# A diffusion-backbone layer on one Trainium2 core: the order of the loads in its first merge block, the place of a pool, and the queue of the result's loads and stores

## The chip, the core and the metric

The kernel runs on one core of a Trainium2 chip. Five engines run their own streams of instructions: PE (TensorE, the matmuls), DVE (VectorE), ACT (ScalarE), POOL (GpSimd) and SP (SyncE, which here only issues DMAs). An engine takes its instructions in the order in which they were built into its stream, so an instruction that waits holds everything behind it on that engine. A DMA is issued by an engine (here SP and POOL), its bytes move on 16 DMA engines that all issuers share, and the instruction that needs the data waits on a semaphore.

The metric is device time in microseconds (us). Before the change three runs gave 3526.43, 3517.88 and 3511.94 us; the median is 3517.88 us.

## What is computed

One layer on 2048 latent tokens and 256 context tokens of width 1024, float32 (cut from the reference):

```python
hx = modulate(rmsnorm(x, norm1_g), sh1, sc1)
px = hx @ w_in                                        # recurrent | Fourier | gate columns
qx = rwkv_inputs(centred_shift(px[..., :RWKV_COLS]), lp)
yx, _, _ = bidir_wkv(qx, Sf, Sb, True)                # RWKV-7 scan, both directions
fx = fourier_latent(px[..., FOURIER_START:GATE_START], rows)
r  = rwkv_output(yx, qx, lp)                          # group norm, bonus, gate, @ w_up_r
m  = sigmoid(gate_f) * (fx @ w_up_f) + sigmoid(gate_r) * r
x  = x + ga1 * (m @ w_out)
hx2 = modulate(rmsnorm(x, norm2_g), sh2, sc2)
x  = x + ga2 * ((silu(gate) * up) @ w_down)           # gate, up = split(hx2 @ w_gu)
return rmsnorm(x, final_norm_g)
```

## The kernel before

Products keep float32 accuracy by splitting each operand into a high part and a remainder and adding three matmuls (`mm3`, lines 269 to 271: high by high, high by low, low by high). A weight comes in as `wraw` (line 261, SP), ACT makes `whi` from it (line 262) and DVE `wlo` (line 263). One matmul is 128x128 by 128x512.

The part up to the end of the scan is the same in both kernels. The stages that the change touches come after it:

- **Merge.** The 2048 tokens are four blocks of 512, taken in the order 1, 2, 0, 3. For each block `normed(n, j)`, four times, loads 128 tokens of the two scan results and what goes with them (`gny`, `gnb`, `gnv`, `sg`), sums them (POOL), normalises them (DVE for even j, a long row of ACT instructions for odd j), transposes them on PE (`gnt`, line 1232), multiplies by the gate (`gng`, line 1239) and splits the result into `oh` and `ol`. For the first block this normalisation is done earlier; only `ready(i)` loads its results (`gnb`, line 1196). `c_merge(n, ct)`, eight times a block, loads a weight `wr` of 512 KB (two places) and three tiles of 256 KB, `gr`, `gf`, `fm` (eight places of the tag `t2` for all of them), does 12 matmuls into `pr`, and puts the merged value into `mh` and `ml`. `c_out(n, ct)`, eight times a block, multiplies that by `w_out` (24 matmuls into `po`) and adds the residual `x1` (the DMA `x`, 512 KB for two). The output product of one block is built beside the merge of the next.
- **Operands of the feed-forward product.** `Operands.build(k)` reads `x1` back, applies the second norm and makes seven sums and differences (`hB`/`lB`, `hT`/`lT`), in tiles of `t2`; POOL makes the last `lT` (line 1318). Six products of the first three up steps, `early`, need only the first two of the seven and are done at the end of this stage.
- **Up**, twice. For each of 22 steps four weights `wA` (line 1404, SP) are combined on DVE (line 1409) into seven, each split and multiplied; results go to DRAM from POOL (`u_dr`, line 1432).
- **Down**, four times, one for each block. 22 steps of `wraw<-w_down`, `u_`, 8 banks of PSUM (`pd`, line 1484). At its end the eight banks are read with `x1f` (loaded from DRAM, line 1508), the row sum gives `rsf`, and DVE multiplies (line 1524) into the result, which is stored (`out_T`, line 1525). The second and fourth down follow a first and a third at once. During the first, POOL loads and builds the operands of the second up.

Tiles live in pools that are laid out on a stack. The tag `t2` of the merge lives in the pool `eb`, beside the second set of `m` and `x1` tiles. The pool `ff`, which holds `wA`, `u_` and the like, is opened where `eb` was, so the first instruction that writes into `ff` waits for the last readers of what `eb` held there.

What sets the order: each engine's stream is laid out by a scheduler, which simulates a timeline and takes the instruction that it finds ready first; the source's order counts only for instructions that go through the `Pinned` engines of lines 50 to 59 (`PE`, `DV`, `AC`, `GP`, `SY`), which keep it among themselves. Pinned instructions carry line 59 in the profile, whoever calls them. Before the change the loads of the merge were laid out by the scheduler:

```python
for ct in range(8):
    c_merge(0, ct)
    if ct in (4, 6):
        normed(1, ct // 2 - 2)
normed(1, 2)
normed(1, 3)
```

Of the kernel before, what the change touches and what calls it, by code (L numbers as in the profile page):

```python
# [7 lines left out]
F32 = mybir.dt.float32  # L8
# [32 lines left out]
def layer_kernel(ctx: ExitStack, tc, I, out_T, dbg=None):  # L41
# [210 lines left out]
    nc.gpsimd.memset(emb, -math.log(2.0))  # L252
    wah = cst.tile([128, 16], F32, name="wah")
    nc.vector.tensor_scalar(out=wah, in0=vec[:, V_W0:V_W0 + 16], scalar1=0.5, scalar2=None, op0=ALU.mult)
    def load_w(src, K, other=None):
        hi = wp.tile([128, KT, 128], F32R, tag="whi", name="whi", bufs=2)
        lo = wp.tile([128, KT, 128], F32R, tag="wlo", name="wlo", bufs=2)
        for k0 in range(0, K, 4):
            k1 = min(K, k0 + 4)
            raw = other() if other and k0 else wp.tile([128, 4, 128], F32, tag="wraw", name="wraw", bufs=RW)[:, 0:k1 - k0, :]  # L260
            nc.sync.dma_start(raw, src[:, k0:k1, :])
            nc.scalar.activation(out=hi[:, k0:k1, :], in_=raw, func=AF.Copy)  # L262
            nc.vector.tensor_tensor(out=lo[:, k0:k1, :], in0=raw, in1=hi[:, k0:k1, :].bitcast(F32), op=ALU.subtract)  # L263
        return hi, lo
# [919 lines left out]
    def gt(tag, b, shape=(128, 512), dt=F32):  # L1184
        return GN[0].tile(list(shape), dt, tag=tag, name=tag, bufs=b)
# [7 lines left out]
    def ready(i):  # L1193

        yb = gt("gnb", 4)
        nc.sync.dma_start(yb, yb_dr[128 * i:128 * i + 128, :])
        oh_split(0, i, yb)

    def normed(n, j):

        i = 4 * TB[n] + j
        y, yb, v_, sg, s8 = gt("gny", 3), gt("gnb", 4), gt("gnv", 2), gt("sg", 3, (128, 128)), gt("s8", 4, (128, 4, 8))
        nc.sync.dma_start(y, y_dr[0][128 * i:128 * i + 128, :])
        nc.sync.dma_start(yb, y_dr[1][128 * i:128 * i + 128, :])
        nc.sync.dma_start(v_, bv_dr[i].rearrange("p t s -> p (t s)"))
        nc.sync.dma_start(sg, sg_dr[:, CTX + 128 * i:CTX + 128 * i + 128])
# [36 lines left out]
    def c_merge(n, ct):  # L1243
        tb = TB[n]
        if ct == 0:
            MHL[n] = [EP[n % 2].tile([128, KT, 512], F32R, tag=f"m{y}", name=f"m{y}{tb}") for y in "hl"]
        (mh, ml), (oh, ol) = MHL[n], OHL[n]
        w = gt("wr", 2, (128, KT, 128), F32R)
        nc.sync.dma_start(w.bitcast(F32), wr_dr[ct])
        gr, gf, fm = t2("gr"), t2("gf"), t2("fm")  # L1250
        nc.sync.dma_start(gr, g_dr[8 + ct][:, 512 * tb:512 * tb + 512])
        nc.sync.dma_start(gf, g_dr[ct][:, 512 * tb:512 * tb + 512])
        nc.sync.dma_start(fm, fm_dr[ct][:, 512 * tb:512 * tb + 512])
        nc.scalar.activation(out=gf, in_=gf, func=AF.Copy, bias=1.0)
        nc.gpsimd.tensor_tensor(out=gf, in0=gf, in1=fm, op=ALU.mult)
        pr = pcx.tile([128, 512], F32, tag="cx", name="pr")
        mm3(pr, (w[:, 0:4, :], w[:, 4:8, :]), lambda k: oh[:, k, :], lambda k: ol[:, k, :], 4, 512)
        nc.vector.scalar_tensor_tensor(out=gr, in0=gr, scalar=1.0, in1=pr, op0=ALU.add, op1=ALU.mult)
        nc.vector.tensor_tensor(out=gr, in0=gr, in1=gf, op=ALU.add)
        split(mh[:, ct, :], ml[:, ct, :], gr)  # L1260

    def c_out(n, ct, acc_):
        tb = TB[n]
        mh, ml = MHL[n]
        if ct == 0:
            X1T[n] = EP[n % 2].tile([128, KT, 512], F32, tag="x1", name=f"x1_{tb}")
            ACC[n] = acc_()
        x1, acc = X1T[n], ACC[n]
        if ct % 2 == 0:
            nc.sync.dma_start(x1[:, ct:ct + 2, :], XTv[:, ct:ct + 2, CTX + 512 * tb:CTX + 512 * tb + 512])  # L1270
        w = load_w(I["w_out"][ct], KT, (lambda: gt("wo", 3, (128, 4, 128))) if n < 3 else None)
        po = pcx.tile([128, 512], F32, tag="cx", name="po")
        mm3(po, w, lambda k: mh[:, k, :], lambda k: ml[:, k, :], KT, 512)
        nc.vector.scalar_tensor_tensor(out=x1[:, ct, :], in0=po, scalar=ga1h[:, ct:ct + 1], in1=x1[:, ct, :], op0=ALU.mult, op1=ALU.add)
        nc.gpsimd.dma_start(x1_dr[:, ct, 512 * tb:512 * tb + 512], x1[:, ct, :])
        q = t2("sqk") if ct else acc
        nc.scalar.activation(out=q, in_=x1[:, ct, :], func=AF.Square)
        if ct:
            nc.gpsimd.tensor_tensor(out=acc, in0=acc, in1=q, op=ALU.add)
# [56 lines left out]
            ready(ct)  # L1336
    for ct in range(8):
        c_merge(0, ct)
        if ct in (4, 6):
            normed(1, ct // 2 - 2)  # L1340
    normed(1, 2)
    normed(1, 3)
    acc_ = lambda: t2("acc")
    for ct in range(2):
        c_out(0, ct, acc_)
# [15 lines left out]
    for ct in range(8):  # L1361
        c_out(3, ct, lambda: fh.tile([128, 512], F32, tag="rs", name="acc3", bufs=3))
        if ct == 0:
            out_stats(2, t2("rs"))
        if ct % 2:
            ops0.build(ct // 2)
    early = {}
    for f in range(3):
        w = load_w(I["w_gu"][f], KT)
        early[f] = {}  # L1370
        for m, o in enumerate(OPS[:2]):
            ps = pcx.tile([128, 512], F32, tag="cx", name="e" + o) if f < 2 else pmm.tile([128, 512], F32, tag="mm", name="e" + o)
            mm3(ps, [x[:, 4 * m:4 * m + 4, :] for x in w], lambda k: ops0.X[o][0][:, k, :], lambda k: ops0.X[o][1][:, k, :], 4, 512)
            early[f][o] = ps
    eps.close()


    ff = fst.enter_context(tc.tile_pool(name="ff", bufs=1, side="right"))

    def tmp(name):  # L1380
        return ff.tile([128, 512], F32, tag="t2", name=name, bufs=8)

    def raw_(name):
        return ff.tile([128, 512], F32, tag="raw", name=name, bufs=6)
# [76 lines left out]
    def down(tb, between=None):  # L1461
# [41 lines left out]
        for ct in range(8):  # L1503
            for f in (FT - 2, FT - 1):
                mm(f, ct)
            x1 = tmp("x1f")
            X1.append(x1)
            nc.sync.dma_start(x1, x1_dr[:, ct, t0:t0 + 512])
            nc.vector.scalar_tensor_tensor(out=x1, in0=PD[ct], scalar=ga2h[:, ct:ct + 1], in1=x1, op0=ALU.mult, op1=ALU.add)
            q = ff.tile([128, 512], F32, tag="sq", name="sqf", bufs=2) if ct else acc  # L1510
            nc.scalar.activation(out=q, in_=x1, func=AF.Square)
            if ct:
                nc.vector.tensor_tensor(out=acc, in0=acc, in1=q, op=ALU.add)
# [6 lines left out]
        for k in range(KT):  # L1520
            if last:
                (nc.gpsimd if k in (1, 4, 6) else nc.vector).tensor_tensor(out=X1[k], in0=X1[k], in1=rs, op=ALU.mult)
            else:
                nc.vector.scalar_tensor_tensor(out=X1[k], in0=X1[k], scalar=vec[:, V_GF + k:V_GF + k + 1], in1=rs, op0=ALU.mult, op1=ALU.mult)
            nc.sync.dma_start(out_T[128 * k:128 * k + 128, t0:t0 + 512], X1[k])

    up(0, ops0.X, early, lambda: out_stats(3, fh.tile([128, 512], F32, tag="rs", name="rs3", bufs=3)))
    ops1 = Operands(1, raw_, nc.gpsimd)
# [112 lines left out]
```

## Time and profile before

| | |
|---|---|
| median of three runs | 3517.88 us (3511.94 to 3526.43) |
| the profiled execution's own time | 3525.59 us |
| its span, first to last instruction | 3523.8 us |
| mean granted clock of PE | 0.959 |
| busy in the span | PE 3259.1 us, PE's weight loads 2692.1, DVE 2359.7, ACT 1603.5, POOL 712.7 |
| first merge block | 1764.3 to 1837.1 us |
| other merge blocks, operands, early products | 1837.1 to 2141.8 us |
| first up, first down, second down | 2153.9 to 2571.4, from there to 2713.7, from 2721.3 on |

Busy times overlap, so they don't add up to the span. The granted clock is a share of full speed: 1.00 is 2.4 GHz and 0.50 is 1.2 GHz; a mean between them means that the stretch had some of both. A row of the table of stretches shows where PE stood still: the length of the stretch less PE's busy time.

### The profile page before, as it was taken

The page shows a single profiled execution, that of the slowest core. Times are in us where ns is not written, and L with a number is a line of the kernel's source. Part 1 is how long each engine was busy: PE and PEld are TensorE (multiplying, and loading weights), DVE is VectorE, ACT ScalarE, POOL GpSimd, SP SyncE. Part 2 cuts the span into 40 slices and gives each one's busy share as a digit, 9 for nine tenths or more (in the row PEclk, how much of TensorE's full clock was granted, in tenths as well). Part 3 has the DMA queues.
Part 4 walks back from the last instruction along what each step waited for, and adds up shares of the span by engine and source line. Part 5 has one row for each costly group of instructions (what it writes and reads, how often), then busy time and mean ns, then how long its engine had stood idle before and what let it go on. Part 6 is the DMA issues. An engine that isn't in the chain of part 4 may idle for free.

```text
span 3523.8 us, 56518 instructions
## 1 busy us (share of the span) xinstructions
PE 3259.1 (92%) x20598; PEld 2692.1 (76%) x20598; DVE 2359.7 (67%) x4404; ACT 1603.5 (46%) x3092; POOL 712.7 (20%) x1118
## 2 busy tenths in 40 slices
PE   7999899999988888999969998999998999999987
PEld 6787777877877777777747876888877888888865
DVE  7678578757657777666666568777774397776354
ACT  4768466557543444444555344333353343333332
POOL 2133232323222343222123342000120000000000
PEclk9999999999999888999979999999999999999998
DMA  6344655544444665777588864222264432223452
GB/s 230 107 158 157 209 196 168 186 127 157 156 167 134 169 186 167 209 237 208 163 303 299 243 197 130 90 84 84 84 207 161 137 117 81 84 86 105 148 171 89
DMA packets 309924, 563.37 MB, mean 160 GB/s; under 512 B 91632, under 2 KB 103152, under 8 KB 309648
## 3 DMA queue, kind: packets, MB, share of 16 engines
q1 hardware_dynamic: 265744, 420.66, 37.4%
q0 software_dynamic: 43904, 139.12, 12.2%
q8 instruction: 163, 2.67, 0.3%
q14 instruction: 113, 0.93, 0.1%
HBM read 406.93 MB, written 152.71 MB: 159 GB/s over the span
## 4 chain that ended last, share of the span: by engine, by line
PE 35%; issue 11%; DMA 7%; DVE 5%; ACT 1%; POOL 1%; SPq 0%; DVEq 0%; POOLq 0%; ACTq 0%
PE pd L1484 11%; PE pT L269 3%; PE pT L270 2%; PE pT L271 2%; PE pB L271 2%; PE pB L269 2%; PE pB L270 2%; PE pf L59 1%; PE po L269 1%; PE po L270 1%; PE po L271 1%; DMA wraw<-w_down 1%; PE xr L59 1%; DMA tb_dr<-Q 1%; PE qk L59 1%
## 5 line engine op out<-in xcount | busy, mean ns | idle before, releaser
L263 DVE TENSOR_TENSOR wlo<-wraw,whi 128x512 fp32r<-128x512 f32 x438 | 298.0, 705 | 366.0 <-ACT whi L262 357.3
L262 ACT ACTIVATE whi<-wraw 128x512 fp32r<-128x512 f32 x438 | 262.4, 626 | 446.9 <-PE pd L1484 192.3
L1484 PE MATMUL pd<-uh,whi 128*128 128x512 f32 x704 | 278.8, 396 | 23.8 <-ACT whi L262 22.1
L1484 PE MATMUL pd<-ul,whi 128*128 128x512 f32 x704 | 277.0, 393 | 0.0
L269 PE MATMUL pxps<-hh,whi 128*128 128x512 f32 (+2 forms) x720 | 249.7, 347 | 8.8 <-ACT whi L262 6.3
L1484 PE MATMUL pd<-uh,wlo 128*128 128x512 f32 x704 | 252.6, 391 | 1.4 <-DVE wlo L263 1.2
L270 PE MATMUL pxps<-hl,whi 128*128 128x512 f32 (+2 forms) x720 | 246.0, 343 | 5.3 <-DVE hl L59 4.1
L271 PE MATMUL pxps<-hh,wlo 128*128 128x512 f32 (+2 forms) x720 | 245.2, 346 | 4.8 <-DVE wlo L263 4.6
L269 PE MATMUL fps<-hh,whi 128*128 128x512 f32 (+1 forms) x688 | 248.9, 362 | 0.3
L271 PE MATMUL fps<-hh,wlo 128*128 128x512 f32 (+1 forms) x688 | 244.6, 356 | 0.8 <-DVE wlo L263 0.8
L270 PE MATMUL fps<-hl,whi 128*128 128x512 f32 (+1 forms) x688 | 243.2, 354 | 0.0
L1422 DVE TENSOR_TENSOR u<-u,pT 128x512 f32<-128x512 f32 x172 | 118.0, 686 | 127.4 <-PE pT L271 126.0
L1484 PEld LDWEIGHTS pd<-uh,whi 128*128 128x128 f32 x704 | 133.9, 190 | 58.7 <-ACT whi L262 27.7
L59 DVE TENSOR_TENSOR tm<-Q,AI 128x126 f32<-128x126 f32 (+22 forms) x558 | 150.2, 269 | 36.9 <-DMA AI<-ab_dr 20.4
L59 DVE TENSOR_TENSOR Q<-Q,tm 128x126 f32<-128x126 f32 (+22 forms) x558 | 154.0, 276 | 20.2
L269 PEld LDWEIGHTS pxps<-hh,whi 128*128 128x128 f32 x720 | 137.2, 191 | 29.1 <-ACT whi L262 8.6
L270 PEld LDWEIGHTS pxps<-hl,whi 128*128 128x128 f32 x720 | 137.0, 190 | 27.8 <-DVE hl L59 6.5
L1484 PEld LDWEIGHTS pd<-uh,wlo 128*128 128x128 f32 x704 | 132.7, 189 | 30.2 <-DVE wlo L263 2.6
L1484 PEld LDWEIGHTS pd<-ul,whi 128*128 128x128 f32 x704 | 133.9, 190 | 27.8
L271 PEld LDWEIGHTS pxps<-hh,wlo 128*128 128x128 f32 x720 | 136.8, 190 | 22.2 <-DVE wlo L263 6.3
L269 PEld LDWEIGHTS fps<-hh,whi 128*128 128x128 f32 x688 | 130.7, 190 | 22.6 <-issue 3.4
L271 PEld LDWEIGHTS fps<-hh,wlo 128*128 128x128 f32 x688 | 130.4, 190 | 22.7 <-issue 2.7
(760 smaller groups left out, 8673.6 us busy)
## 6 DMA issues: line engine op xcount, KB each, us to landing
wraw<-w_in SPq DMA_DIRECT2D x210, 256.0 KB, 3.2
wraw<-w_down SPq DMA_DIRECT2D x176, 256.0 KB, 2.9
wA<-w_gu SPq DMA_DIRECT2D x176, 256.0 KB, 2.7
BD<-bd_dr SPq DMA_DIRECT2D x36, 512.0 KB, 7.1
KR<-kr_dr SPq DMA_DIRECT2D x36, 512.0 KB, 7.8
wada<-w_ada SPq DMA_DIRECT2D x32, 512.0 KB, 4.0
wf<-wf_dr SPq DMA_DIRECT2D x32, 512.0 KB, 6.9
wr<-wr_dr SPq DMA_DIRECT2D x32, 512.0 KB, 6.2
```

The source lines that it names most:

```text
L59: return lambda *a, **k: tc.keep_in_program_order(f(*a, **k))
L262: nc.scalar.activation(out=hi[:, k0:k1, :], in_=raw, func=AF.Copy)
L263: nc.vector.tensor_tensor(out=lo[:, k0:k1, :], in0=raw, in1=hi[:, k0:k1, :].bitcast(F32), op=ALU.subtract)
L269: nc.tensor.matmul(ps, wh[:, k, :], xh(k), start=start and k == 0, stop=False)
L270: nc.tensor.matmul(ps, wh[:, k, :], xl(k), start=False, stop=False)
L271: nc.tensor.matmul(ps, wl[:, k, :], xh(k), start=False, stop=stop and k == K - 1)
L1422: nc.vector.tensor_tensor(out=o, in0=x, in1=y, op=ALU.add)
L1484: nc.tensor.matmul(PD[ct], x[:, ct, :], y, start=f == 0 and i == 0, stop=f == FT - 1 and i == 2)
```

## The change

Three things change. The first is the order of the loads in the first merge block: the loads of `c_merge(0, ct)`, of `ready`, of the next block's `normed` (now in `block_load`) and the weights and residual of the first two output steps go through `SY`, in the order in which the source calls them. The second is the place of `t2`: it gets a pool of its own, `et`, which stays open, so that `eb` holds only the `m` and `x1` tiles, and is closed ahead of the early products. The third is the queue of the result's loads and stores: `x1f` is loaded, and `out_T` of the first three downs stored, by POOL.

```diff
@@ load_w @@
-    def load_w(src, K, other=None):
+    def load_w(src, K, other=None, sy=nc.sync):
...
-            nc.sync.dma_start(raw, src[:, k0:k1, :])
+            sy.dma_start(raw, src[:, k0:k1, :])
@@ pools @@
+    et = fst.enter_context(tc.tile_pool(name="et", bufs=1, side="right"))
     eps = ctx.enter_context(ExitStack())
     eb = eps.enter_context(tc.tile_pool(name="eb", bufs=1, side="right"))
...
     def t2(name):
-        return eb.tile([128, 512], F32, tag="t2", name=name, bufs=8)
+        return et.tile([128, 512], F32, tag="t2", name=name, bufs=8)
@@ ready @@
-        nc.sync.dma_start(yb, yb_dr[128 * i:128 * i + 128, :])
+        SY.dma_start(yb, yb_dr[128 * i:128 * i + 128, :])
@@ normed @@
+    LD = {}
+
+    def block_load(n, j, sy=nc.sync):
+        i = 4 * TB[n] + j
+        y, yb, v_, sg = gt("gny", 3), gt("gnb", 4), gt("gnv", 2), gt("sg", 3, (128, 128))
+        sy.dma_start(y, y_dr[0][128 * i:128 * i + 128, :])
+        sy.dma_start(yb, y_dr[1][128 * i:128 * i + 128, :])
+        sy.dma_start(v_, bv_dr[i].rearrange("p t s -> p (t s)"))
+        sy.dma_start(sg, sg_dr[:, CTX + 128 * i:CTX + 128 * i + 128])
+        LD[n, j] = y, yb, v_, sg
...
+        if (n, j) not in LD:
+            block_load(n, j)
+        y, yb, v_, sg = LD[n, j]
@@ c_merge @@
+        sy = nc.sync if n else SY
         w = gt("wr", 2, (128, KT, 128), F32R)
-        nc.sync.dma_start(w.bitcast(F32), wr_dr[ct])
+        sy.dma_start(w.bitcast(F32), wr_dr[ct])
...
@@ c_out @@
+        sy = nc.sync if n or ct > 1 else SY
...
@@ the first block @@
         c_merge(0, ct)
-        if ct in (4, 6):
-            normed(1, ct // 2 - 2)
-    normed(1, 2)
-    normed(1, 3)
+        if ct in (1, 2, 4, 6):
+            block_load(1, {1: 0, 2: 1, 4: 2, 6: 3}[ct], SY)
+        if ct in (3, 4, 6, 7):
+            normed(1, {3: 0, 4: 1, 6: 2, 7: 3}[ct])
@@ before and after the early products @@
+    eps.close()
+    ff = fst.enter_context(tc.tile_pool(name="ff", bufs=1, side="right"))
     early = {}
...
-    eps.close()
-
-
-    ff = fst.enter_context(tc.tile_pool(name="ff", bufs=1, side="right"))
-
-    def tmp(name):
-        return ff.tile([128, 512], F32, tag="t2", name=name, bufs=8)
+
+
+
+    tmp = t2
@@ down @@
-            nc.sync.dma_start(x1, x1_dr[:, ct, t0:t0 + 512])
+            nc.gpsimd.dma_start(x1, x1_dr[:, ct, t0:t0 + 512])
...
-            nc.sync.dma_start(out_T[128 * k:128 * k + 128, t0:t0 + 512], X1[k])
+            (nc.sync if last else nc.gpsimd).dma_start(out_T[128 * k:128 * k + 128, t0:t0 + 512], X1[k])
```

In `c_merge` the three loads of `gr`, `gf` and `fm`, and in `c_out` the load of `x` and the call of `load_w`, use `sy` in the same way. Because lines were added, line numbers of the changed kernel are higher: the weights of up are line 1415 in place of 1404, `x1f` 1519 in place of 1508, `out_T` 1536 in place of 1525, the builds 1321 to 1333 in place of 1309 to 1321.

The first place is SP's stream at the start of the first merge block, just behind the load of `g` and the four loads of `gnb<-yb_dr`. Before:

```order
L1249 DMA wr<-wr_dr_122 128x1024
L1249 DMA wr<-wr_dr_123 128x1024
L1203 DMA gny<-y_dr_94 128x512
L1205 DMA gnv<-bv_dr 128x512
L1206 DMA sg<-sg_dr 128x128
L1203 DMA gny<-y_dr_94 128x512
L1205 DMA gnv<-bv_dr 128x512
L1251 DMA gr<-g_dr_81 128x512
L1252 DMA gf<-g_dr_73 128x512
L1253 DMA fm<-fm_dr_98 128x512
L1251 DMA gr<-g_dr_82 128x512
L1252 DMA gf<-g_dr_74 128x512
```

and with the change (loads through `SY` stand under line 59):

```order
L59 DMA wr<-wr_dr_122 128x1024
L59 DMA gr<-g_dr_81 128x512
L59 DMA gf<-g_dr_73 128x512
L59 DMA fm<-fm_dr_98 128x512
L59 DMA wr<-wr_dr_123 128x1024
L59 DMA gr<-g_dr_82 128x512
L59 DMA gf<-g_dr_74 128x512
L59 DMA fm<-fm_dr_99 128x512
L59 DMA gny<-y_dr_94 128x512
L59 DMA gnb<-y_dr_95 128x512
L59 DMA gnv<-bv_dr 128x512
L59 DMA sg<-sg_dr 128x128
```

A merge step's four operands now follow each other. In the rows behind these, the kernel before has `x`, `wo`, `wraw` of `w_out` between the operands of the eight steps; the changed one has seven loads of `x` (after the rows shown), one `block_load` after the operands of the third, fifth and seventh step, and the weights of `w_out` behind the eighth.

The second place is the end of the operands and the start of up. On SP, before:

```order
L261 DMA wraw<-w_gu 128x512
L1309 DMA x__22015<-x_dr 128x512
L261 DMA wraw<-w_gu 128x512
L261 DMA wraw<-w_down 128x512 x4
L1404 DMA wA<-w_gu 128x512 x4
L261 DMA wraw<-w_down 128x512 x2
L1404 DMA wA<-w_gu 128x512 x11
```

and with the change:

```order
L261 DMA wraw<-w_gu 128x512
L1321 DMA x__22018<-x_dr 128x512
L1415 DMA wA<-w_gu 128x512 x2
L261 DMA wraw<-w_gu 128x512
L1415 DMA wA<-w_gu 128x512 x3
L261 DMA wraw<-w_down 128x512 x2
L1415 DMA wA<-w_gu 128x512 x3
L261 DMA wraw<-w_down 128x512 x2
L1415 DMA wA<-w_gu 128x512
```

The loads of `wA` moved ahead of the last weight of the early products (`wraw<-w_gu`) and of the first weights of down (`wraw<-w_down`). On DVE, with the change (`lB` and `lT` belong to the last build, `wS`/`wA` of line 1420 are the combined weights):

```order
L1420 TENSOR_TENSOR wS<-wA 128x512
L1330 TENSOR_TENSOR lB_0_21562<-x__22018,hB_0_21561 128x512
L1433 TENSOR_TENSOR c_22167<-u_22153,eB_22068 128x512
L1420 TENSOR_TENSOR wA<-wA 128x512
L1333 TENSOR_TENSOR x__22010<-x__22010,x__22006 128x512
L263 TENSOR_TENSOR wlo<-wraw,whi 128x512 x2
L1330 TENSOR_TENSOR lT_0_21556<-t_22022,hT_0_21555 128x512
L1420 TENSOR_TENSOR wA<-wS,wA 128x512
L1438 SCALAR_TENSOR_TENSOR tg<-tg,c_22167 128x512
L1333 TENSOR_TENSOR x__22006<-x__22018,x__22010 128x512
L1330 TENSOR_TENSOR lT_0_21558<-x__22010,hT_0_21557 128x512
L1420 TENSOR_TENSOR wA<-wA 128x512
```

The four combinations of line 1409 (now 1420), which stood behind all rows of the last build and of the early products, now stand between them.

The third place is the end of the first down, where the second follows. On SP, before:

```order
L1475 DMA u__26939<-u_dr_19104 128x512
L1475 DMA u__26979<-u_dr_19105 128x512
L1525 DMA out_T<-x1f 128x512 x4
L1508 DMA x1f<-x_dr 128x512
L1525 DMA out_T<-x1f 128x512 x2
L1508 DMA x1f<-x_dr 128x512
L1525 DMA out_T<-x1f 128x512 x2
L261 DMA wraw<-w_down 128x512
L1508 DMA x1f<-x_dr 128x512
L261 DMA wraw<-w_down 128x512
```

and with the change:

```order
L1486 DMA u__26942<-u_dr_19104 128x512
L1486 DMA u__26982<-u_dr_19105 128x512
L261 DMA wraw<-w_down 128x512 x2
L1486 DMA u__27022<-u_dr_19106 128x512
L1486 DMA u__27062<-u_dr_19107 128x512
L261 DMA wraw<-w_down 128x512 x3
L1486 DMA u__27102<-u_dr_19108 128x512
```

The rows of `out_T` and `x1f` are gone from between the weights. They stand on POOL, with the change, at the same place (`lT` is the last row of the builds of the second up):

```order
L1330 TENSOR_TENSOR lT_1_25460<-x__26268,hT_1_25459 128x512
L1536 DMA out_T<-x1f 128x512 x4
L1519 DMA x1f<-x_dr 128x512
L1536 DMA out_T<-x1f 128x512 x2
L1519 DMA x1f<-x_dr 128x512
L1536 DMA out_T<-x1f 128x512
L1519 DMA x1f<-x_dr 128x512
L1536 DMA out_T<-x1f 128x512
L1519 DMA x1f<-x_dr 128x512 x5
```

and, where the first down begins and POOL builds those operands:

```order
L1443 DMA u_dr_19116<-u_25384 128x512
L1519 DMA x1f<-x_dr 128x512 x5
L1333 TENSOR_TENSOR t_25886<-x__25882,x__25874 128x512
L1321 DMA x__26065<-x_dr 128x512
L1519 DMA x1f<-x_dr 128x512
L1443 DMA u_dr_19116<-c_25404 128x512
L1519 DMA x1f<-x_dr 128x512
L1321 DMA x__26069<-x_dr 128x512
L1333 TENSOR_TENSOR x__25878<-x__25878,x__25870 128x512
L1321 DMA x__26073<-x_dr 128x512
L1321 DMA x__26077<-x_dr 128x512
```

In the kernel before the rows of `x1f` are not among these; the store of `u` is followed at once by `t`. Five loads of `x1f` now stand between them.

## Rows read from the trace of the kernel before

**Rows 1.** The page: its head, and busy time by engine.
```profile
span 3523.8 us, 56518 instructions
...
PE 3259.1 (92%) x20598; PEld 2692.1 (76%) x20598; DVE 2359.7 (67%) x4404; ACT 1603.5 (46%) x3092; POOL 712.7 (20%) x1118
```

**Rows 2.** Stretches: length; busy PE, PEld, DVE, ACT, POOL; clock, DMA share, GB/s.
```profile
1764.30:1837.10 72.80, 37.97 (x145) 30.00 (x146) 43.78 (x74) 38.67 (x122) 20.69 (x16) 0.72 0.92 334
1772.00:1824.00 52.00, 29.23 (x108) 22.42 (x108) 32.35 (x53) 26.16 (x79) 15.46 (x11) 0.72 1.04 382
1837.10:1908.00 70.90, 70.90 (x337) 59.09 (x335) 48.59 (x80) 36.64 (x89) 28.87 (x26) 1.00 0.78 257
1908.00:1917.00 9.00, 2.27 (x11) 2.21 (x11) 5.89 (x11) 6.30 (x25) 2.11 (x2) 0.65 1.04 397
2115.90:2141.80 25.90, 20.37 (x72) 13.86 (x72) 24.81 (x31) 17.16 (x29) 12.34 (x10) 0.93 0.38 122
2141.80:2153.90 12.10, 0.03 (x1) 0.06 (x1) 6.58 (x11) 4.75 (x8) 1.69 (x1) 0.69 0.63 196
2571.40:2575.00 3.60, 0.08 (x2) 0.08 (x1) 2.75 (x3) 1.91 (x4) 3.31 (x5) 1.00 1.01 342
2713.70:2721.30 7.60, 0.02 (x2) 0.01 (x1) 0.72 (x2) 1.26 (x2) 0.00 (x0) 0.67 0.92 270
2721.30:2728.00 6.70, 6.70 (x19) 5.32 (x20) 1.36 (x2) 0.63 (x1) 0.00 (x0) 0.61 0.99 364
3388.40:3395.70 7.30, 0.07 (x1) 0.07 (x1) 0.78 (x2) 1.26 (x2) 0.00 (x0) 0.76 0.96 315
```

**Rows 3.** What PE waited for in the first block: total, times, longest.
```profile
PE pr L269 <- DMA wr<-wr_dr: 12.1, 2, 9.8
PE gnt L1232 <- ACT gny L1221: 6.3, 1, 6.3
```

**Rows 4.** DMAs issued from 1764 to 1826 us: size, median time to landing.
```profile
x<-xT SPq DMA_DIRECT2D x8, 512.0 KB, 7.6
...
gnb<-y_dr SPq DMA_DIRECT2D x7, 256.0 KB, 5.4
gny<-y_dr SPq DMA_DIRECT2D x6, 256.0 KB, 5.9
...
wo<-w_out SPq DMA_DIRECT2D x5, 256.0 KB, 7.3
...
wraw<-w_out SPq DMA_DIRECT2D x2, 256.0 KB, 6.5
```

**Rows 5.** What SP's queue waited for from 1760 to 1837 us.
```profile
SPq L1206 <- PE gng L1239: 4.9, 1, 4.9
SPq L1249 <- PE gnt L1232: 3.6, 1, 3.6
SPq L626 <- DMA fm_dr<-ev: 3.5, 1, 3.5
```

**Rows 6.** Timeline ahead of up, SP's DMAs: start, duration.
```profile
2143.92 1.75 SPq L1404 DMA_DIRECT2D wA<-w_gu  x4
```

**Rows 7.** Timeline there, DVE; in brackets the idle time before, and its releaser.
```profile
2150.96 0.69 DVE L1409 TENSOR_TENSOR wS<-wA 128x512 f32<-128x512 f32 x1 [1.64 <-DMA wA<-w_gu]
```

**Rows 8.** Timeline at the end of the first down, DVE.
```profile
2710.87 1.28 DVE L263 TENSOR_TENSOR wlo<-wraw,whi 128x512 fp32r<-128x512 f32 x2
```

**Rows 9.** Timeline there, SP's DMAs.
```profile
2715.62 0.52 SPq L261 DMA_DIRECT2D wraw<-w_down  x1
```

**Rows 10.** The page's DMA issues over the whole program.
```profile
wraw<-w_down SPq DMA_DIRECT2D x176, 256.0 KB, 2.9
```

**Rows 11.** DMAs issued from 2563 to 2578 us.
```profile
u_dr<-u POOLq DMA_DIRECT2D x1, 256.0 KB, 5.2
```

**Rows 12.** Timeline at the start of the first down, POOL.
```profile
2564.25 0.56 POOL L1432 DMA_DIRECT2D u_dr<-u  x1 [2.66 <-DVE u L1431]
2566.73 3.25 POOL L1321 TENSOR_TENSOR t<-x__25879,x__25871 128x512 f32<-128x512 f32 x1 [1.92 <-ACT x__25879 L1311]
```

More of the change, by code (lines that the diff above doesn't have):

```diff
@@ L1195, in ready @@
         yb = gt("gnb", 4)
-        nc.sync.dma_start(yb, yb_dr[128 * i:128 * i + 128, :])
+        SY.dma_start(yb, yb_dr[128 * i:128 * i + 128, :])
         oh_split(0, i, yb)
-    def normed(n, j):
[L1201 to L1206, printed above, removed]
+    LD = {}
[7 more added lines that the diff above has]
+        LD[n, j] = y, yb, v_, sg
+    def normed(n, j):
+        if (n, j) not in LD:
+            block_load(n, j)
+        y, yb, v_, sg = LD[n, j]
+        s8 = gt("s8", 4, (128, 4, 8))
         nm, ss, nb = s8[:, 0, :], s8[:, 1, :], s8[:, 2, :]
@@ L1247, in c_merge @@
         (mh, ml), (oh, ol) = MHL[n], OHL[n]
+        sy = nc.sync if n else SY
         w = gt("wr", 2, (128, KT, 128), F32R)
-        nc.sync.dma_start(w.bitcast(F32), wr_dr[ct])
+        sy.dma_start(w.bitcast(F32), wr_dr[ct])
         gr, gf, fm = t2("gr"), t2("gf"), t2("fm")
-        nc.sync.dma_start(gr, g_dr[8 + ct][:, 512 * tb:512 * tb + 512])
-        nc.sync.dma_start(gf, g_dr[ct][:, 512 * tb:512 * tb + 512])
-        nc.sync.dma_start(fm, fm_dr[ct][:, 512 * tb:512 * tb + 512])
+        sy.dma_start(gr, g_dr[8 + ct][:, 512 * tb:512 * tb + 512])
+        sy.dma_start(gf, g_dr[ct][:, 512 * tb:512 * tb + 512])
+        sy.dma_start(fm, fm_dr[ct][:, 512 * tb:512 * tb + 512])
         nc.scalar.activation(out=gf, in_=gf, func=AF.Copy, bias=1.0)
@@ L1268, in c_out @@
         x1, acc = X1T[n], ACC[n]
+        sy = nc.sync if n or ct > 1 else SY
         if ct % 2 == 0:
-            nc.sync.dma_start(x1[:, ct:ct + 2, :], XTv[:, ct:ct + 2, CTX + 512 * tb:CTX + 512 * tb + 512])
-        w = load_w(I["w_out"][ct], KT, (lambda: gt("wo", 3, (128, 4, 128))) if n < 3 else None)
+            sy.dma_start(x1[:, ct:ct + 2, :], XTv[:, ct:ct + 2, CTX + 512 * tb:CTX + 512 * tb + 512])
+        w = load_w(I["w_out"][ct], KT, (lambda: gt("wo", 3, (128, 4, 128))) if n < 3 else None, sy)
         po = pcx.tile([128, 512], F32, tag="cx", name="po")
```

## The prediction

> **What bounds the kernel now.** I read the page's busy times first. PE is busy 3259.1 of 3523.8 us, 92% [rows 1], so PE sets the pace and an edit counts only where it shortens a time in which PE stands still. Everything up to 1764.3 us is the same in both kernels. Second I read the table of stretches for such times behind that point; the idle time is the length less PE's busy time [rows 2]. The first merge block has 72.80 - 37.97 = 34.8 us of it, the change to up 12.1, the start of the first down 3.6 at most, the two changes from one down to the next 7.6 and 7.2. These five places, 65 us together, are all that the change touches and that PE feels. The stretch behind the first block, for one, has no idle time in 70.9 us.
>
> Third I read what ended each of them. In the first block PE waits for `wr` and for `gny` [rows 3], links of chains that start with a load, and from 1772 to 1824 us the DMA engines are full (share 1.04 at 382 GB/s [rows 2]). So bytes are the limit there for 52 us, and in the last 13 us the chain through ACT. At the change to up, SP asks for `wA` only at 2143.92, 2.1 us after PE's last matmul [rows 6], and DVE starts on it at 2150.96 [rows 7]. At the change between downs DVE gives back the places of `wraw` at 2710.87 + 1.28 = 2712.15 at the latest [rows 8], but SP issues the load at 2715.62 [rows 9], behind `out_T` and `x1f`.
>
> **The change part by part.**
>
> *First block.* The loads through SY ask first for what the merge products need. Of the issues up to 1826 us these move behind the last merge operand: one `x` of 512 KB (eight before, seven now), five `wo` and two `wraw` of `w_out`, two `gny` and three `gnb` of the block after the next (the next one needs four of each) [rows 4]. That is 0.52 + 12 x 0.262 = 3.7 MB, at 382 GB/s 9.6 us. Besides, SP stood 3.5 us for the landing of a store of `fm_dr` [rows 5] that had two loads of `w_out` in front of it; these are gone, and I count 1.5 us of the 3.5. Sum -11. The bounds: -17, if in addition `gnt` no longer waits for `gny`, whose row of waits is 6.3 us [rows 3]; and 0, if the deferred bytes are paid for later. For that they need idle DMA time: from 1837.1 to 1908.0 the share is 0.78, so 15.6 us are idle, and 9.6 us fit [rows 2]. But the next 9 us are full (1.04) and PE is busy for 2.27 of them, so a part may come back there; -11 holds by the nearer row, and the rest of the merge I take as 0, from -4 to +7 (one more such hole of 9.00 - 2.27 = 6.7).
>
> *Place of `t2`.* `wA` waited for the last reader of a `t2` tile, POOL's last `lT`. Now it waits for the last reader of `x1` alone, the store and the square of the last output step, which come before the early products. Its loads move ahead of 2141.8, so the DMA leaves the path (its share there is 0.38 [rows 2]). What is late next is DVE: it is busy 24.81 of the 25.9 us of the early products [rows 2], and the combined weights, five operations of 0.69 us [rows 7] up to the first split weight, now stand between the rows of the last build and delay it by 3.4 us. So of the 12.1 us some 3.5 stay: -8.6, and with a shorter stop a little less time at the lower clock (0.69 in the stop): -9. Bounds: -14, the whole 12.1 and 2 us of clock; -3, if DVE's rows delay the early products by as much as they save behind them.
>
> *Queue of the result's loads and stores.* With `out_T` and `x1f` off SP's queue, `wraw` is issued at the release of its place, 2711.5 for the first (half of the 1.28 us of two operations [rows 8]), 4.1 us sooner than 2715.62 [rows 9]. The transfer itself stays slow, since the 4 MB of `out_T` and `x1f` still move. So 7.6 - 4.1 = 3.5 us stay and the gain is 4.1; behind the hole PE has 19 matmuls in 6.7 us at a clock of 0.61 [rows 2], where at full clock one takes 70.9 / 337 = 0.21 us on the mean of the stretch at 1837 us; (6.7 / 0.21 - 19) x 0.21 = 2.7 us are lost to the clock, and I count 1 of them back. That is -5, and the same at the second place (7.30 us, 0.07 busy [rows 2]): -10. Bounds: -17, both holes and clock wholly gone; 0, if the loads only share the same bytes per second sooner.
>
> Over the program `wraw<-w_down` lands 2.9 us after its issue [rows 10]; here PE goes on 5.7 us after it, at 2721.3 [rows 2, 9], one conversion by ACT included: the traffic costs some 2 us whoever issues it. The Trainium skill ("DMA: Bandwidth & Descriptors", section "Issuing engines are not separate DMA queues") says that transfers from all issuers run on the same 16 engines, and that spreading them only saves time on the sequencer. By that rule alone this part would be worth nothing; but the trace shows that it is SP's standing in line, 2711.5 to 2715.62, that counts here, which is the part that the rule leaves.
>
> *Start of the first down.* SP is rid of `x1f`, but POOL now issues five of them between the store of `u` and `t`, and the fifth waits for that store's landing, 5.2 us [rows 11]. So `t`, which started at 2566.73, starts behind 2564.25 + 5.2 = 2569.45 at the earliest [rows 12]: 2.7 us late, and ACT's `hT<-t` with it, on whose stream the `whi` stands that PE waits for. Against that the weights come sooner, and ACT does them ahead of the last `hT`. From -3.5 (the hole of 3.6 [rows 2] gone) to +4; I take -1.
>
> The stores from POOL behind up's `u_dr`, and the 32 loads, need about 0.56 us of POOL each [rows 12]; POOL is busy 20% of the span [rows 1], which hides them.
>
> Sum: -11 + 0 - 9 - 10 - 1 = -31 us. The profiled execution took 3525.59 us, 1.8 more than its span [rows 1]; it would take 3494.6. It is 7.7 us above the median of 3517.88, and the median goes to 3487.
>
> **The rivals.**
>
> *The bytes come back.* The deferred bytes have to land before the second block is through; if the hole at 1908 us grows by what the first block gains, 11 us are gone: 3517.88 - 20 = 3498. For: share 1.04 there. Against: 15.6 idle us before it, and PE busy without a gap until then [rows 2].
>
> *The change between downs gains nothing.* POOL issues `out_T` and `x1f` at the same time as SP issues `wraw`, and all land in 7 us as before: 3517.88 - 21 = 3497. For: shares of 0.92 and 0.96 in the holes [rows 2]. Against: `wraw` would stand first and not last.
>
> *The place of `t2` does not do what it says.* If DVE, not the load, ends the wait for up, the sum is -22, 3496. For: DVE's 24.81 of 25.9 us. Against: DVE idle for 1.64 us just before `wS` [rows 7].
>
> *SP stands in fixed order: slower.* In the pinned order a `block_load` whose place isn't free holds all operands behind it. SP's waits for PE were 4.9 and 3.6 us, for one `sg` and one `wr` [rows 5]; if each of the four block loads costs both, 34 us of standing are set against the gain of 11, +23, and the weights of `w_out`, later by that, open the hole of 6.7 us at each of the three blocks behind: +20. With the other terms, -20, that is +23: 3541. It decides once SP's lag exceeds the 15.6 idle us. For: seven loads of `x`, 3.7 MB, stand in front of the third step's weight. Against: those waits came when SP had run ahead and PE was busy with the steps before.
>
> **How the numbers follow.** The forecast has a chance of 0.55, the bytes that come back 0.15, no gain between downs 0.12, the place of `t2` 0.06, the fixed order 0.12 (in full strength or half). What a measurement tells from no change is 0.5%, 17.6 us, so faster means below 3500.3. The forecast's own range by its bounds is 3470 to 3502. Faster: nearly all of 0.55, two thirds of the next three cases (all stand 2 to 4 us from the bound), 0.73 together. Slower: half of the last, 0.06; the same: 0.21. The low end is 3466, where all four terms reach their lower bounds (-17 - 14 - 17 - 3.5 = -51.5); the high end is 3512, where the first two rivals come together and part of the term on up fails as well.
>
> **What would show it.** First block: `po` starts near 1826 in place of 1837, with `wr` and `gr` of each step in a row and the share still near 1; if the hole at 1908 is longer than 9 us, the bytes came back. Up: `wA` issued before PE's last early product, and the first `pT` some 3.5 us behind it, released by DVE. Downs: `wraw` issued at the release by `wlo`, holes of 3 to 4 us. First down: `t` late by some 3 us. I am wrong if the sum over those five holes doesn't fall by about 30 us, and by much if PE gets holes between 1837 and 2115 that weren't there, or if SP waits for PE in the first block for longer than 8.5 us in all.

## The result, and the profile after

The changed kernel takes 3505.65 us in the median of 20 runs (3490.08 to 3513.58), the kernel before 3525.28 us in the median of 20 (3511.68 to 3535.59). The ratio is 0.9944 with a 95% interval from 0.9931 to 0.9958: 0.56% or 20 us faster, where 31 us were forecast. The page of the changed kernel begins

```profile
span 3510.5 us, 56527 instructions
...
PE 3268.3 (93%) x20598; PEld 2697.7 (77%) x20598; DVE 2358.7 (67%) x4404; ACT 1606.1 (46%) x3092; POOL 744.9 (21%) x1174
```

The two profiled spans differ by 13.3 us, but that is not the effect. The scan's last matmul ended at 1764.3 us before and at 1772.8 us after, although both kernels have the same instructions up to there. So the stages are compared from the scan's end on. The table is read off PE's timeline (start of the first or end of the last matmul of a kind), so the first down begins here with its first `pd`, at 2560.4 us before, and not with PE's stop at 2571.4; the last three columns are experiments with one part each, told below.

| stage, us | before | changed | order of loads alone | place of t2 alone | queue alone |
|---|---|---|---|---|---|
| scan's end to first `po` | 72.8 | 63.7 | 65.3 | 73.6 | 73.2 |
| first to last `po` | 278.8 | 283.7 | 283.3 | 276.2 | 280.4 |
| last `po` to first `pT` of up | 38.0 | 30.9 | 38.4 | 29.7 | 38.8 |
| first up | 406.5 | 404.6 | 406.2 | 405.4 | 405.8 |
| first and second down | 262.0 | 258.4 | 260.7 | 262.5 | 256.0 |
| second up | 419.8 | 419.8 | 419.8 | 419.8 | 419.8 |
| third and fourth down | 254.8 | 252.6 | 253.9 | 255.8 | 250.5 |
| last `pd` to the end | 26.9 | 24.1 | 26.7 | 26.7 | 23.8 |
| all behind the scan | 1759.5 | 1737.8 | 1754.3 | 1749.7 | 1748.4 |

Behind the scan the changed kernel is 21.7 us shorter. The table of stretches of the changed kernel answers to [rows 2]; its columns are the length, the busy time of PE, PEld, DVE, ACT and POOL, PE's granted clock, the DMA share and GB/s:

```profile
1772.80:1836.40 63.60, 34.26 (x132) 25.90 (x132) 36.45 (x62) 29.74 (x87) 18.57 (x15) 0.83 1.00 360
1836.40:2120.10 283.70, 268.63 (x1189) 220.98 (x1189) 178.83 (x275) 141.01 (x331) 108.29 (x97) 0.95 0.76 241
2120.10:2151.00 30.90, 22.05 (x73) 14.75 (x73) 30.62 (x41) 21.66 (x36) 15.19 (x10) 0.89 0.49 159
...
2708.00:2710.60 2.60, 0.62 (x3) 0.19 (x1) 0.69 (x1) 1.26 (x2) 2.31 (x5) 1.00 0.94 230
2716.30:2720.00 3.70, 0.12 (x2) 0.07 (x1) 0.08 (x1) 0.74 (x2) 1.07 (x2) 0.95 1.04 397
...
3379.90:3383.50 3.60, 0.02 (x1) 0.00 (x0) 0.71 (x2) 1.26 (x2) 2.09 (x4) 1.00 0.91 300
3389.20:3392.20 3.00, 0.14 (x2) 0.07 (x1) 0.09 (x1) 0.75 (x2) 0.54 (x1) 0.98 1.01 363
```

The first block still runs its DMA engines full (share 1.00). The stop of 12.1 us ahead of up is gone, but the early products in front of it take 30.9 us, with DVE busy for 30.62 of them. Each change between downs has two stops of PE (stretches in which it does nothing), 2 to 3.6 us each, where one of over 7 stood; the clock stays near 1.00 in them, where it was 0.67 and 0.76.

What PE waited for in the changed kernel's first block, beside [rows 3]:

```profile
PE pr L269 <- DMA gr<-g_dr: 9.0, 1, 9.0
PE gnt L1242 <- DVE gny L1239: 9.0, 2, 7.1
PE po L269 <- ACT whi L262: 5.7, 1, 5.7
PE pr L269 <- DMA wr<-wr_dr: 4.4, 6, 1.5
PE gnt L1242 <- ACT gny L1231: 1.4, 2, 1.0
```

The waits for `wr` fell from 12.1 to 4.4 us and the one for ACT's `gny` from 6.3 to 1.4. A new one stands at the end: `po` waits 5.7 us for `whi`, the weights of `w_out`, which now come last. SP's waits there answer to [rows 5]; it waited for PE once, for 1.5 us:

```profile
SPq L626 <- DMA fm_dr<-ev: 1.8, 1, 1.8
...
SPq L59 <- PE pr L271: 1.5, 1, 1.5
```

### The profile page after: what moved, and what is told of

It reads as the page before. It is cut to its first block, busy times and chain, and to the rows that moved or that the text cites. A ratio compares the mean times of both kernels' runs of the same rounds, so it can differ in the third digit from the quotient of the medians.

```text
span 3510.5 us, 56527 instructions
## 1 busy us (share of the span) xinstructions
PE 3268.3 (93%) x20598; PEld 2697.7 (77%) x20598; DVE 2358.7 (67%) x4404; ACT 1606.1 (46%) x3092; POOL 744.9 (21%) x1174
## 4 chain that ended last, share of the span: by engine, by line
PE 45%; DMA 5%; DVE 4%; issue 3%; ACT 1%; POOL 0%; SPq 0%; DVEq 0%; POOLq 0%; ACTq 0%
PE pd L1495 11%; PE pT L269 5%; PE pT L270 5%; PE pT L271 5%; PE pB L269 3%; PE pB L270 3%; PE pB L271 3%; PE po L269 1%; DMA wraw<-w_down 1%; PE po L270 1%; PE po L271 1%; PE pf L59 1%; PE qk L59 1%; PE pr L269 1%; DVE wlo L263 1%
## 5 line engine op out<-in xcount | busy, mean ns | idle before, releaser
L269 PE MATMUL pxps<-hh,whi 128*128 128x512 f32 (+2 forms) x720 | 250.5, 348 | 8.9 <-ACT whi L262 6.6
L269 PEld LDWEIGHTS pxps<-hh,whi 128*128 128x128 f32 x720 | 137.4, 191 | 29.7 <-ACT whi L262 9.1
## 6 DMA issues: line engine op xcount, KB each, us to landing
wraw<-w_in SPq DMA_DIRECT2D x210, 256.0 KB, 3.2
wA<-w_gu SPq DMA_DIRECT2D x176, 256.0 KB, 2.7
wraw<-w_down SPq DMA_DIRECT2D x176, 256.0 KB, 2.9
```

What stands on the lines that cost most here:

```text
L269: nc.tensor.matmul(ps, wh[:, k, :], xh(k), start=start and k == 0, stop=False)
```

## The experiments

Eleven kernels ran. A ratio is against the kernel before on the same chip, with its 95% interval.

**Each part alone.** Three kernels have the kernel before and one part of the change.

> Kernel before, with the fixed order of the loads in the first merge block alone. Theory 1 (the three parts add up, each as the trace of the changed kernel shows it): from the scan's last matmul to the first po 64 us in place of 72.8, then from the first po to the last 284 us in place of 279, the change to up and the downs as before; in all about 4 us faster. Rival (the bytes put off come back whole): the same first stretch, but the second longer by all of the 9 us; 0.

> Kernel before, with the pool of t2 and the earlier place of ff alone. Theory 1 (DVE is what the change to up now waits for): PE's stop of 12.1 us ahead of up is gone, the early products take 31 us in place of 26, and from the last po to the first pT 31 us in place of 38: 7 us faster. Rival (the longer early products of the changed kernel come from its other parts): the stop gone, the early products 26 us, 12 us faster.

> Kernel before, with x1f and out_T on GpSimd's queue alone. Theory 1 (wraw no longer stands behind them, but all bytes still land in the same time): at each change between downs two stops of PE of 2 to 4 us each in place of one of 7.6 and smaller ones; 3 us each and 6 us in all faster. Rival (the loads of x1f hold POOL's t at the start of the first down): the stop of 3.5 us there grows to 6 or more, and 3 us at most are left.

Measured: 0.9977 (0.9961 to 0.9993) for the order of the loads, 0.9984 (0.9965 to 1.0002) for the place of `t2`, 0.9988 (0.9972 to 1.0004) for the queue. The product is 0.9949, beside 0.9944 for all three, so the parts add up; the last two intervals hold 1. The stages tell more: behind the scan the parts gain 5.2, 9.8 and 11.1 us in their traces, 26.1 together, somewhat more than the 21.7 of the whole. For the queue the trace says 11 us and the ratio 4 (up to 10 by its interval); a trace is one execution, and which of the two is nearer the ratios leave open.

The order of the loads does what theory 1 says: 7.5 us less to the first `po`, 4.5 more from there to the last. The place of `t2`: no stop, early products 29.8 us in place of 25.9, 8.3 us less in all (7 expected), and so the longer early products are its own price. The queue: 6.0 and 4.3 us less in the two pairs of downs (3 expected for each), and 3.1 at the end, which no theory had. Theory 1 had two stops at each change between downs; there is one, of 3.0 and 3.4 us, and behind it none longer than 1 us. The start of the first down did not get slower: PE's stop there is 2.7 us.

**Does DVE set the pace of the early products?** The edit on the changed kernel; `lo` is not made:

```diff
-        w = load_w(I["w_gu"][f], KT)
+        hi = wp.tile([128, KT, 128], F32R, tag="whi", name="whi", bufs=2)
+        for k0 in (0, 4):
+            raw = wp.tile([128, 4, 128], F32, tag="wraw", name="wraw", bufs=RW)
+            nc.sync.dma_start(raw, I["w_gu"][f][:, k0:k0 + 4, :])
+            nc.scalar.activation(out=hi[:, k0:k0 + 4, :], in_=raw, func=AF.Copy)
+        w = hi, hi
```

> Changed kernel; the low part of the weights of the six early products is left out (the high part is used in its place), so DVE has six operations less there. Theory 1 (DVE sets the pace of the early products): from the last po to the first pT 26 us in place of 31. Rival (loads or ACT set it): 30 to 31 us as before.

Measured: 26.9 us from the last `po` to the first `pT` (theory 1: 26), where the other kernels with this place of `t2` have 29.5 to 30.9 (28.5 in one). In the changed kernel PE's waits in that stretch were

```profile
PE eB L271 <- DVE wlo L263: 5.6, 4, 2.0
PE eB L270 <- DVE lB L1330: 1.8, 1, 1.8
PE eB L269 <- ACT whi L262: 1.4, 3, 0.6
```

and without the six operations on DVE

```profile
PE eB L270 <- DVE lB L1330: 3.2, 2, 3.1
PE eB L269 <- ACT hB L1329: 2.4, 2, 1.8
```

So DVE sets most of the pace, and the last build's own rows, on DVE and ACT, are next.

**Are bytes the limit of the first block?** The seven early loads of `x` go behind the merge operands:

```diff
         if ct % 2 == 0:
-            sy.dma_start(x1[:, ct:ct + 2, :], ...
+            (SY if n < 2 else nc.sync).dma_start(x1[:, ct:ct + 2, :], ...
```

> Changed kernel, with all loads of x for the first two blocks in the fixed order too, so that the seven early ones (3.7 MB) go behind the operands of the eight merge steps. Theory 1 (bytes limit the first block: 3.7 MB at 382 GB/s are 9.6 us): the last pr ends 8 to 10 us sooner after the scan than 58 us; po then waits for its weights and starts 6 to 9 us sooner than 63.7. Rival (the chain from gny to ol, or two places of wr, sets the pace): 0 to 3 us sooner.

and, in a second kernel, the first weights of `w_out` come earlier as well:

```diff
         c_merge(0, ct)
+        if ct == 5:
+            W0.append(load_w(I["w_out"][0], KT, lambda: gt("wo", 3, (128, 4, 128)), SY))
```

> As x_late, and the weights of the first output step are loaded ahead of the operands of the last two merge steps. Theory 1 (po waits 5.7 us only because its weights are last in line): PE's stop ahead of po falls below 2 us, the merge products end 1 to 2 us later, po starts 3 us sooner than in x_late. Rival (all is one queue of bytes, whatever their order): po starts within 1 us of x_late.

Measured: 0.9923 (0.9897 to 0.9949) and 0.9932 (0.9909 to 0.9956), not to be told from the changed kernel's 0.9944. In the trace of the first the last `pr` ends 54.9 us after the scan (58.0 in the changed kernel, 60.4 with the order of loads alone), and `po` starts after 58.3: 5.4 us sooner, less than the 6 to 9 of theory 1 and more than the 0 to 3 of the rival. The last `pr` ended 3.1 us sooner than in the changed kernel, where theory 1 had 8 to 10. Its first block and PE's waits in it:

```profile
1763.00:1821.20 58.20, 33.03 (x132) 25.21 (x132) 34.96 (x63) 29.62 (x86) 19.40 (x15) 0.85 0.90 308
```

```profile
PE pr L269 <- DMA wr<-wr_dr: 11.4, 5, 2.6
PE pr L269 <- DVE ol L275: 9.4, 1, 9.4
PE po L269 <- ACT whi L262: 3.3, 1, 3.3
```

The DMA share is 0.90, so bytes no longer fill the whole block; PE waits five times, up to 2.6 us, for `wr`, which has two places. Both theories hold a part. With the weights earlier the stop ahead of `po` is gone and `po` starts after 56.2 us, 2 us sooner; but from the first to the last `po` it takes 288.6 us, 5 more, with a new stop of 3.3 us ahead of a `pr` 17 us into it. In this trace, what is taken from the one stop comes back behind it.

**What makes the two stops between downs?** The first attempt fixed the order of all that a down loads on SP:

```diff
-            w = load_w(I["w_down"][f], KT)
+            w = load_w(I["w_down"][f], KT, None, SY)
...
-            nc.sync.dma_start(r, u_dr[f][:, t0:t0 + 512])
+            SY.dma_start(r, u_dr[f][:, t0:t0 + 512])
...
+            if f >= FT - 10:
+                x1 = tmp("x1f")
+                X1.append(x1)
+                SY.dma_start(x1, x1_dr[:, len(X1) - 1, t0:t0 + 512])
```

> Changed kernel, with the weights, u_ and x1f of the downs in a fixed order on SP; x1f is loaded beside the weights of the last ten steps of its own down, out_T stays on GpSimd's queue. Theory 1 (the stops of 2.0 and 3.6 us between downs, and 3.5 at the first, are the loads of x1f landing among the weights): the second stop at each change gone, the first 1 to 2 us, the one at the first down under 1: 8 to 11 us faster than the changed kernel. Rival (the stops are the 5.4 us of eight multiplications on DVE ahead of wlo): 0 to 3 us faster.

> As x1f_late, and the stores of out_T of the first and third down also go to SP, one behind the weights of each step from the third on of the next down. Theory 1 (stores and loads share the 16 engines, and stores compete as loads do): no stop over 1 us from DMA between downs; 2 to 4 us faster than x1f_late. Rival (DVE's multiplications hold wlo): a stop of 2 us or more stays, within 1 us of x1f_late.

Measured: 1.0103 (1.0080 to 1.0125) and 1.0133 (1.0109 to 1.0156). Both are slower; neither theory had that. Each pair of downs takes 28 to 34 us longer than in the changed kernel, all along its length. The cause is in the order: the scheduler had SP load `u_` six to seven steps ahead of the weights, and the fixed order put each `u_` behind its own weights. ACT then waits for it and holds the `whi` behind it. From the timeline of ACT in `x1f_late`,

```profile
2614.28 0.63 ACT L274 ACTIVATE uh<-u__25995 128x512 fp32r<-128x512 f32 x1 [5.54 <-DMA u__25995<-u_dr]
2614.81 1.14 ACT L262 ACTIVATE whi<-wraw 128x512 fp32r<-128x512 f32 x2
...
2625.75 0.63 ACT L274 ACTIVATE uh<-u__26112 128x512 fp32r<-128x512 f32 x1 [3.89 <-DMA u__26112<-u_dr]
```

beside the changed kernel at the same time, where `uh` follows at once:

```profile
2617.26 0.63 ACT L262 ACTIVATE whi<-wraw 128x512 fp32r<-128x512 f32 x1 [1.43 <-DMA wraw<-w_down]
2617.80 0.62 ACT L274 ACTIVATE uh<-u__26190 128x512 fp32r<-128x512 f32 x1
```

The second attempt fixes the order of `x1f` alone (the last three lines above, without the first two edits).

> Changed kernel; only x1f is in a fixed order on SP, beside the weights of the last ten steps of its own down, while the weights and u_ are left to the scheduler (in x1f_late they were fixed too, and u_ lost its lead of six steps). Theory 1 (the stops of 2.0 and 3.6 us between downs and of 3.5 at the first are the loads of x1f among the weights): the halves with these stops take 128 us in place of 132, the first half of the first down 123 to 124 in place of 126.7; 8 to 10 us faster than the changed kernel behind the scan. Rival (the slow thing is DVE's eight multiplications ahead of wlo): 0 to 2 us faster.

Measured: 0.9942 (0.9922 to 0.9963), the ratio of the changed kernel, and 1730.1 us behind the scan, 7.7 less than in the changed kernel's trace; 5.8 of these are in the two pairs of downs, the rest in stages that the edit does not touch. So the slowdown of `x1f_late` is gone, and a gain over the changed kernel stands in the trace alone. The second halves of the pairs (the second and the fourth down) take 130.0 and 128.3 us (131.7 and 132.8 in the changed kernel). The second stop is gone at both places, as theory 1 says; the first is 4.2 us in place of 2.0 at the one place and 2.8 in place of 3.6 at the other, and the one at the start of the first down stays (3.8 us), which it does not say. Of the first stop, from DVE's and SP's timelines and the table of stretches of this kernel:

```profile
2683.40 5.39 DVE L1541 SCALAR_TENSOR_TENSOR x1f<-x1f,vec,rsf 128x512 f32<-128x512 f32 x8
2688.70 1.29 DVE L263 TENSOR_TENSOR wlo<-wraw,whi 128x512 fp32r<-128x512 f32 x2
```

```profile
2689.42 1.45 SPq L261 DMA_DIRECT2D wraw<-w_down  x2
```

```profile
2691.50:2695.70 4.20, 0.06 (x1) 0.00 (x0) 0.69 (x1) 1.26 (x2) 0.00 (x0) 1.00 0.89 302
```

The weight is issued at its place's release, which waits behind the eight multiplications, and its transfer runs among the stores (share 0.89): it lands 5.5 us after its issue, where 2.9 is the median of the program [rows 10]. So the first stop hangs on the rival's DVE, which sets the time of issue, and on the stores; no run separates the two.

The loads of `x1f` had the second stop. The two weights issued ahead of it, changed kernel (2711.2 to 2713.5 us) and `x1f_late3` (2696.0 to 2697.8):

```profile
wraw<-w_down SPq DMA_DIRECT2D x2, 256.0 KB, 7.7
```

```profile
wraw<-w_down SPq DMA_DIRECT2D x2, 256.0 KB, 2.7
```

Slow weights need not make a stop, though: in the kernel with the queue alone the two weights at that place land 6.8 and 6.2 us after their issue, and PE waits 1.0 us.

**Loads or stores in line?** The changed kernel with `out_T` back on SP:

```diff
-            (nc.sync if last else nc.gpsimd).dma_start(out_T[128 * k:128 * k + 128, t0:t0 + 512], X1[k])
+            nc.sync.dma_start(out_T[128 * k:128 * k + 128, t0:t0 + 512], X1[k])
```

> Changed kernel with out_T of all downs back on SP's queue and only x1f on GpSimd's. Theory 1 (what held wraw on SP was x1f waiting for the landing of out_T; the stores alone are issued by the time at which DVE gives back wraw's place): the halves with the change between downs take 131 to 133 us as in the changed kernel. Rival (the eight stores in line hold wraw as well): 134 us or more, near the 135 of before.

Measured: 0.9945 (0.9926 to 0.9963); 133.0 and 132.0 us for the halves with the change, as theory 1 says. The stores are issued by the time at which the weight's place is free, as SP's timeline shows:

```profile
2687.72 4.25 SPq L1536 DMA_DIRECT2D out_T<-x1f  x6
2692.07 2.00 SPq L261 DMA_DIRECT2D wraw<-w_down  x2
```

So the move of `x1f` alone ends the standing in line. PE's first stop is 6.9 us all the same (4.3 at the second place), near the 7.6 of before and not the 2.0 of the changed kernel. The two weights go out among the eight stores and the loads of `x1f`; DMAs issued from 2692.07 to 2694.1 us, and the stretch of the stop:

```profile
wraw<-w_down SPq DMA_DIRECT2D x2, 256.0 KB, 7.9
```

```profile
2693.80:2700.60 6.80, 0.00 (x0) 0.00 (x0) 0.69 (x1) 1.26 (x2) 3.22 (x6) 0.82 0.99 340
```

An early issue is thus not enough; what flies along counts as well. Whether moving `out_T` too is worth a microsecond these halves do not tell.

**A better kernel.** `x_late` and `x1f_late3` together:

> x_late and x1f_late3 together. Theory 1 (the places are independent): the sum of both against the changed kernel, some 4 and 8 us: behind the scan 1725 to 1728 us in place of 1737.8, about 0.989 of the kernel before. Rival (what is gained in one place is lost to the clock or in the next): no better than x_late, 0.992.

Measured: 0.9934 (0.9917 to 0.9950), median 3491.41 us where the kernel before has 3516.15 on that chip, and 1726.4 us behind the scan, the shortest of all (theory 1: 1725 to 1728). The ratio misses the 0.989 of theory 1 and is no better than `x_late`'s, as the rival says. It beats the kernel before; against the changed kernel the intervals overlap, and only the trace, 11.4 us shorter behind the scan, speaks for it. On the same chip `x1f_late3` has 3492.02 us and `x1f_pool`, which differs from the changed kernel in the queue of the stores alone, 3495.93: the three are not to be told apart.

## Why the prediction was right, and where its sizes were off

The time lies in the range and the direction holds. The forecast was 31 us, the runs give 20. The time of 3505.65 us is 19 us above the 3487 of the forecast and above its own range of 3470 to 3502; 7 of the 19 come from the kernel before, whose median of 20 runs is higher than that of the three I had. It lies in the whole range, up to 3512, by the width that was there for the rivals, and that is in part luck. By the sign that I had named, the idle time of PE in the five places fell from 65 us to 45 (29.3, 0, 3.5, 5.6 and 6.5), by 20 and not by 30.

One trace of a stage differs from another by some us with nothing changed in it: from the first to the last `po` 278.8, 276.2 and 280.4 us in the three kernels with the old order of the loads. So the sizes below, from the two first traces, stand beside means over all traces that have a part in just this form, against the three without it. By these means the first block gains 4.3 us (seven traces), the place of `t2` 8.6 (nine), the queue 7.3 in the downs and 2.7 at the end (five): 23 in all, where the ratio's interval is 15 to 24 us. Nearly all that is missing from the 31 is missing in the first block. By its steps:

- **First block, forecast -11: the mis-sized term, -4.2 in all.** The steps on the bytes and on `fm_dr` held: SP's wait there fell from 3.5 us [rows 5] to 1.8, where I counted 1.5 us, and with 3.7 MB fewer in front the last `pr` ended 15 us sooner (58.0 us after the scan in place of 73.0). It failed at what is late next, since the deferred weights of `w_out` are what `po` needs first: 5.7 of those us went into a stop ahead of `po`, and -9.1 were left. Then "the rest of the merge I take as 0, from -4 to +7" measured +4.9. The hole near 1908 did not grow (5.74 us where it was 5.76), so the rival that put the return there is wrong in its place. The return has two other sources. PE has 11 more matmuls behind the first `po` (1189 for 1178), at 0.22 us each 2.4 us: work that moved, not time that was saved. And behind its new stop PE starts at the low clock (0.51, the level of 1.2 GHz). The first 6 us behind the first `po`, changed kernel and before:

```profile
1836.50:1842.50 6.00, 6.00 (x14) 4.65 (x15) 5.97 (x12) 4.73 (x13) 1.57 (x2) 0.51 0.84 289
```

```profile
1837.10:1843.10 6.00, 6.00 (x28) 4.99 (x27) 5.86 (x11) 3.31 (x8) 1.29 (x1) 1.00 0.58 192
```

  Fourteen matmuls fewer at 0.21 us are 3.0 us. The two add up to 5.4 where 4.9 were measured, but traces of this stage differ by as much, so this split is an estimate. It also isn't all: in `x_late_w`, which has no stop there and starts at a clock of 1.00, the stage is the longest of all.
- **Place of `t2`, forecast -9: measured -7.1, alone -8.3.** DVE is what is late next, as said, but its price is paid at another place. I left 3.5 us of the stop behind the early products; no stop is left, and the early products themselves take 5.2 us more (3.9 alone), 31.1 in place of 25.9 to the end of their last matmul, because PE waits inside them. The size is near the forecast (8.6 on the mean), by another path.
- **Queue, forecast -10: measured -5.8 on PE, and -2.8 at the end.** `wraw` went out at its place's release, as forecast:

```profile
2706.49 0.93 SPq L261 DMA_DIRECT2D wraw<-w_down  x2
```

```profile
2705.77 1.29 DVE L263 TENSOR_TENSOR wlo<-wraw,whi 128x512 fp32r<-128x512 f32 x2
```

  The first stop became 2.0 us, and 3.6 at the second place, where 3.5 was forecast. What I did not see is that the next weights meet the loads of `x1f`, which POOL issues as places come free, for a second stop of 3.6 us (2.9 at the second place); `x1f_late3` shows that it is theirs, and the kernel with the queue alone that it does not always come. The total of this term comes near the forecast only with the 2.8 us at the end, which my sum did not have: that is luck. The rule of the Trainium skill ("DMA: Bandwidth & Descriptors", section "Issuing engines are not separate DMA queues") that all issuers' transfers interleave on the same 16 engines agrees with this second stop (share 1.04 in it) and with the stop of 6.9 us in `x1f_pool` (share 0.99), where the weight was issued half a microsecond after its release. SP's line held the weight for 4.1 us before; but its end shortens the stop only as far as the transfers beside the weight let it. The prediction weighed the line as all that counts, and it is one of two.
- **Start of the first down, forecast -1: 0.** The fifth `x1f` did wait for the store of `u`, but only until 3.6 us after its issue, and `t` started 1.7 us later than before against that store (2.7 forecast). It then took 1.57 us where it had taken 3.25 [rows 12], so ACT lost nothing. PE's stop is 3.45 us, as before. From POOL's timeline:

```profile
2559.73 0.56 POOL L1443 DMA_DIRECT2D u_dr<-u  x1 [2.66 <-DVE u L1442]
2560.29 2.23 POOL L1519 DMA_DIRECT2D x1f<-x_dr  x4
2563.33 0.54 POOL L1519 DMA_DIRECT2D x1f<-x_dr  x1 [0.81 <-DMA u_dr<-u]
2563.89 1.57 POOL L1333 TENSOR_TENSOR t<-x__25882,x__25874 128x512 f32<-128x512 f32 x1
```

- **The rivals.** SP did not stand in the first block: 1.5 us of waiting for PE, where the slower rival needed 34. A fixed order can cost that much, though, by another path: `x1f_late` is 1.0% slower. That the place of `t2` does nothing is refuted by the kernel with this part alone.

## What to carry to other kernels

When loads are put off, look for the first instruction that needs them: a queue of bytes that is full moves its stop to whatever stands last in it, and behind such a stop PE can start at the low clock (0.51 over the first 6 us here). Ahead of a full engine (here DVE), work that is let in earlier is paid for inside the stage that it enters. Taking a load out of a line gains no more than the transfers beside it allow: issued some 4 us sooner, a weight made a stop of 2.0 us in one kernel and of 6.9 in another, where more flew along. Fix the order of the one load that does harm and leave the rest to the scheduler: fixing the weights and `u_` along with `x1f` cost 1.0%, fixing `x1f` alone cost nothing.

## What the runs showed beyond that

The same instructions up to the scan's end took from 1756.8 us to 1773.7 in the 13 traces, a spread of 17 us beside the 20 us that the change is worth. In the two first traces most of it arose between 1122 and 1186 us, where the granted clock was 1.00, 0.99, 0.79 and 0.92 in four stretches before and 0.74, 0.98, 0.67 and 0.70 after. The first up to the end, in contrast, repeats: the second up took 419.8 or 419.9 us in every trace.

The program's end got shorter without an instruction on PE that differs: from the landing of the last `out_T` to the end 4.6 us before, 4.5 with either of the first two parts alone, but 1.5 with the queue alone and 1.8 in the changed kernel. POOL's closing drain took 12.7 us before and 8.9 after; its last DMA was 278 us from the end before and 120 after. In the 13 traces the drain is 12.7 to 13.4 us where that distance is over 270 us and 6 to 9 us where it is under 150. That the distance is the cause was not tested.
